# A decoder step in split fp32 matmuls: weights of two or four blocks interleaved column by column, and an activation stored with tokens in falling order

## The chip, the core and the metric

The kernel runs on one core of one Trainium2 chip, as a single launch. The metric is the time of that launch on the device, in microseconds; the times before are two runs of 599.43 and 599.55 us, median 599.49 us. The five engines of the core appear in the profile under short names: PE (TensorE matmuls), PEld (TensorE weight loads, which can run beside PE's matmuls), DVE (VectorE), ACT (ScalarE), POOL (GpSimd); SP is the queue that issues most of the DMAs.

## The reference

One inference step of two layers, for a prompt of 256 tokens and 8 single sample tokens which share all weights. Each layer has a mixer (one input projection, attention beside a second branch, one output projection) and a feed-forward part with a causal convolution of width 3 on its gate. The feed-forward part is what matters here:

```python
def conv_ffn(x, prev, norm_g, w_gate, w_up, conv_w, conv_b, w_down):
    T = x.shape[1]
    h = rmsnorm(x, norm_g)
    g = h @ w_gate
    g_all = jnp.concatenate([prev, g], axis=1)
    gc = sum(conv_w[i] * g_all[:, i:i + T] for i in range(CONV_W)) + conv_b
    a = jax.nn.gelu(gc) * (h @ w_up)
    return x + a @ w_down, g_all[:, -(CONV_W - 1):]
```

The model width is 1024 and the feed-forward width 2816. All inputs and outputs are fp32.

## The kernel before

Features lie on the 128 partitions and tokens along the free dimension: T = 264 columns, 256 of the prompt and 8 samples. Every weight matrix is cut into blocks of 128 x 128. A block is the stationary operand of a matmul and 128 features x 264 tokens are the moving one, so a weight matrix of 1024 x 2816 is 8 x 22 blocks.

To keep fp32 accuracy, each operand is split into two parts of type fp32r: a high part h, which is the value rounded to fp32r, and a low part l, the rest. A block then takes three matmuls into the same PSUM tile: weight h by activation h, weight h by activation l, weight l by activation h. Each of the three loads its own weights.

The list `_PHASES` (from `_phases`) holds eight phases in the order in which they run, and each phase the order of its blocks: `in0`, `out0`, `ff0`, `dn0`, then the same four of layer 1. `ff0` and `ff1` are the gate and up projections (352 blocks each, 1056 matmuls), `dn0` and `dn1` the down projections (176 blocks each, 528 matmuls). Together these four make 1056 of the 1472 blocks.

On the host, `_pack_weights` lays all blocks out in the order of use, in chunks of 8 or 16 blocks. A chunk lies as 128 rows, one for each partition, and in a row the blocks follow each other, 128 columns each. A DMA brings a chunk into a tile `raw`. `split` takes eight blocks at a time, 128 x 1024: ACT writes the high part into a tile `wh` (line 300) and DVE the low part into `wl` (line 303), three such steps ahead of use. In `run`, block i is then the columns `c` to `c + 128` of both tiles, `c = (i % 8) * P`, and the three matmuls are issued (all through a helper at line 215). When a PSUM tile has its last block, `evac` is called.

In `ffn`, the evacuation of a gate block works out the convolution and the GELU on DVE and ACT; that of an up block multiplies on DVE (line 584) and POOL (line 585), and `halves` (ACT line 445, DVE line 446) splits the product into the tiles `a_h` and `a_l`. These are the moving operand of the down phase, which `hl(act, k)` picks for feature block k. Down phases sum over all 22 feature blocks for each of the 8 output blocks; the outputs are added to the residual `X`.

The order of TensorE's instructions is fixed by hand: they keep the order of the program, and the small matmuls of attention and the other branches are hung between blocks as hooks. The feed-forward phases have almost none.

The line that chooses the block's columns, and the three matmuls, are:

```python
            c = (i % 8) * P
            pe.matmul(o, h[:, c:c + P], xh, start=first, stop=False)
            pe.matmul(o, h[:, c:c + P], xl, start=False, stop=False)
            pe.matmul(o, l[:, c:c + P], xh, start=False, stop=left[m] == 0)
```

Of the kernel before, what the change touches and what calls it, by code (L numbers as in the profile page):

```python
# [18 lines left out]
P = 128  # L19
# [39 lines left out]
def _phases():  # L59
    k8 = list(range(KD))  # L60
    in0 = [(n, t) for n in ("bv", "q", "k", "bu", "v") for t in range(4)]
    q0 = [(m, k) for k in range(KQ) for m in in0[:4]] + [(m, k) for m in in0[:4] for k in range(KQ, KD)]
    in1 = [(n, t) for n in ("u", "q", "k", "v") for t in range(4)]
    m8 = [("o", t) for t in range(8)]
    kb = [4, 5, 6, 7, 0, 1, 2, 3]
    ff = [(n, j) for j in range(NF) for n in ("g", "u")]
    kf = list(range(NF))
    ph = []
    for l, ins in enumerate((in0, in1)):
        ph.append((f"in{l}", _split_order(ins, k8, 4) if l else q0 + [(m, k) for m in in0[4:] for k in k8]))  # L70
        ph.append((f"out{l}", _split_order(m8, kb, 4)))
        ph.append((f"ff{l}", _split_order(ff, k8, 4)))
        ph.append((f"dn{l}", [(m, k) for m in m8 for k in kf]))
    return ph


_PHASES = _phases()
# [5 lines left out]
_COLS = {"in0": {"q": 0, "k": 4, "v": 8, "bu": 12, "bv": 16}, "in1": {"q": 0, "k": 4, "v": 8, "u": 12}}  # L83


def _pack_weights(w_in0, w_out0, w_in1, w_out1, gate, up, down):
    def blocks(w):
        kt, mt = w.shape[0] // P, w.shape[1] // P
        return w.reshape(kt, P, mt, P).transpose(2, 0, 1, 3).reshape(mt * kt, P, P), kt

    mats = {"in0": w_in0, "out0": w_out0, "in1": w_in1, "out1": w_out1}
    for l in range(2):
        mats[f"g{l}"], mats[f"u{l}"], mats[f"dn{l}"] = gate[l], up[l], down[l]
    base, kts, parts, n = {}, {}, [], 0
    for name, w in mats.items():
        b, kts[name] = blocks(w)
        base[name] = n
        parts.append(b)
        n += b.shape[0]
    allb = np.concatenate(parts)  # L100
    idx = []
    for ph, order in _PHASES:
        for (n_, t), k in order:
            if ph in _COLS:
                name, m = ph, _COLS[ph][n_] + t
            elif ph.startswith("ff"):
                name, m = n_ + ph[2], t
            else:
                name, m = ph, t
            idx.append(base[name] + m * kts[name] + k)  # L110
    out, o = [], 0
    for c in _CHUNKS:
        out.append(allb[np.array(idx[o:o + c])].transpose(1, 0, 2).reshape(-1))
        o += c
    return out

# [86 lines left out]
def tile_decoder_step(ctx: ExitStack, tc: tile.TileContext, a):  # L203
# [16 lines left out]
    pe = TensorE()  # L220
# [10 lines left out]
    def f4(name, shape=(P, 4, T), dt=F32):  # L231
        return up.tile(list(shape), dt, tag="u", name=name)

    def mv(name):
        return [f4(f"{name}_{x}", dt=F32R) for x in "hl"]

    def hl(tiles, k):
        return tiles[k // 4][0][:, k % 4, :], tiles[k // 4][1][:, k % 4, :]

    def at(name):  # L240
        return psa.tile([P, 512], F32, tag="at", name=name)
# [13 lines left out]
    def vec(n):  # L255
        o, w = _VEC[n]
        return VEC[:, o:o + w]
# [34 lines left out]
    def split(t):  # L292
        for tt in range(len(splits), min(t + (2 if t == 3 else LOOK), NT - 1) + 1):
            ci = chunk_of[tt]
            for c in range(ci, min(ci + 3, len(_CHUNKS))):
                raw(c)
            o = (tt * 8 - coff[ci]) * P
            src = raws[ci][:, o:o + 8 * P]
            h, l = splits[tt] = wtiles(tt)
            i = s.activation(h, src, AF.Copy)  # L300
            if R0 and tt < 8:
                behind(i, last[0])
            i = v.tensor_tensor(l, src, h.bitcast(F32), ALU.subtract)  # L303
            if tt == 5:
                behind(i, summed)
        return splits[t]

    spare = (32, 40)

    def run(order, rhs, evac, hooks=None):  # L310
        hooks = sorted((hooks or {}).items())
        n = 0
        seen, left, ps = {}, {}, {}
        for m, k in order:
            left[m] = left.get(m, 0) + 1
        for m, k in order:
            i = pos[0]
            pos[0] += 1
            h, l = split(i // 8)
            c = (i % 8) * P  # L320
            if m not in ps:
                ps[m] = at(f"mm{i}") if i in spare else psm.tile([P, 512], F32, tag="mm", name=f"mm{i}")
                first = True
            else:
                first = False
            left[m] -= 1
            o = ps[m][:, :T]
            xh, xl = rhs(m, k)
            pe.matmul(o, h[:, c:c + P], xh, start=first, stop=False)
            pe.matmul(o, h[:, c:c + P], xl, start=False, stop=False)  # L330
            if i == 0:
                busy(128)
            pe.matmul(o, l[:, c:c + P], xh, start=False, stop=left[m] == 0)
            if left[m] == 0:
                evac(m, o)
            n += 1
            while hooks and n >= round(8 * (hooks[0][0] + 1)):
                for f in hooks.pop(0)[1]:
                    f()

    orders = dict(_PHASES)
# [9 lines left out]
    first, o = [], 0  # L351
# [26 lines left out]
    def busy(n):  # L378

        tc.keep_in_program_order(pe.matmul(pw[:, :n], warm[:, :P], warm[:, :n], start=True, stop=True))  # L380
# [46 lines left out]
    def rstd_of(parts, scale, name, pin=False, bank=None, w=None):  # L427
        p = (bank or at)(f"ns_{name}")
        for i, x in enumerate(parts):
            mm = pe.matmul(p[:, :T], ones if w is None else w, x, start=i == 0, stop=i == len(parts) - 1)  # L430
            if pin:
                tc.keep_in_program_order(mm)
        R = sm.tile([P, T], F32, tag="R", name=f"R_{name}", bufs=2)
        s.activation(R, p[:, :T], AF.Ln, bias=epst, scale=scale)
        last[0] = s.activation(R, R, AF.Exp, scale=-0.5)
        return R

# [6 lines left out]
    def halves(h, l, src):  # L444
        s.activation(h, src, AF.Copy)  # L445
        v.tensor_tensor(l, src, h.bitcast(F32), ALU.subtract)  # L446
# [82 lines left out]
    def gelu_set():  # L529
        tc.keep_in_program_order(s.preload_act_table_set("gelu_apprx_tanh_and_others"))  # L530
# [4 lines left out]
    def lnexp():  # L535
        tc.keep_in_program_order(s.preload_act_table_set("natural_log_exp_and_others"))
# [15 lines left out]
    def ffn(l, xg, nrm, down_evac, hooks=None):  # L552
        cw, cb = vec("cw"), vec("cb")
        wc = lambda i, j: cw[:, (l * 3 + i) * NF + j:(l * 3 + i) * NF + j + 1]
        cvo = sm.tile([P, NF, 10], F32, tag="cvo", name=f"cvo{l}", bufs=1)
        act = [mv(f"a{l}_{i}") for i in range((NF + 3) // 4)]
        half = {}
        R = None
        nrm.split()

        def norm():
            nonlocal R
            R = nrm.finish()
            gelu_set()


        def evac(m, o):
            n, j = m
            if n == "g":
                wk = f4(f"wk{l}_{j}", (P, 2, T))  # L570
                C = wk[:, 0, :]
                G = wk[:, 1, :]
                v.tensor_tensor(G, o, R, ALU.mult)
                s.activation(C, G, AF.Identity, scale=wc(2, j), bias=cb[:, l * NF + j:l * NF + j + 1])
                v.scalar_tensor_tensor(C[:, 1:SEQ], G[:, 0:SEQ - 1], wc(1, j), C[:, 1:SEQ], ALU.mult, ALU.add)
                v.scalar_tensor_tensor(C[:, 2:SEQ], G[:, 0:SEQ - 2], wc(0, j), C[:, 2:SEQ], ALU.mult, ALU.add)
                v.tensor_tensor(C[:, SEQ:T], C[:, SEQ:T], C0[:, l, j, :], ALU.add)
                s.activation(cvo[:, j, :], G[:, SEQ - 2:T], AF.Copy)
                s.activation(C, C, AF.Gelu_apprx_tanh)
                half[j] = wk  # L580
            else:
                wk = half.pop(j)
                C, A = wk[:, 0, :], wk[:, 1, :]
                v.tensor_tensor(A, o, R, ALU.mult)  # L584
                g.tensor_tensor(A, A, C, ALU.mult)  # L585
                halves(*hl(act, j), A)

        hk = Hooks()
        hk.at(16 / 8 - 1, norm)
        run(orders[f"ff{l}"], pick(xg), evac, hk)  # L590
        nc.sync.dma_start(a[f"cv{l}"], cvo)
        lnexp()
        run(orders[f"dn{l}"], lambda m, k: hl(act, k), down_evac, hooks)

    def residual(gain, name):
        xg = [mv(f"xg_{name}{i}") for i in range(2)]
# [52 lines left out]
    def pick(xg):  # L649
        return lambda m, k: hl(xg, k)  # L650
# [330 lines left out]
    for n in range(8):  # L981
        hk.at(n, drip_of(kload, 2))
    ffn(0, xg, norm_f, evac, hk)


# [95 lines left out]
    U, A, B = [f4(f"pool{x}", (P, 4, PW + SEQ)) for x in "uab"]  # L1081
# [74 lines left out]
    norm_f = nrm  # L1156
    evac, rest = final()
    ffn(1, xg, norm_f, evac)
    rest()

# [68 lines left out]
```

## Time and profile before

| what | value |
|---|---|
| median of two runs | 599.49 us |
| the profiled execution: its time | 599.23 us |
| the profiled execution: span from first to last instruction | 597.2 us |
| `mm` matmuls in a gate and up phase | 1056 each |
| `mm` matmuls in a down phase | 528 each |
| share of ACT, of DVE in the span | 57%, 71% |
| HBM traffic | 117.65 MB read, 3.96 MB written |

The profile is one execution. A row of a group names the line, the engine, the operation, the tile written and those read, the shape and the count; after the bar stand the busy time in us, the mean length of one in ns, and the idle time of the engine just before them with what ended most of it. A row of the timeline gives the start and the length in us. A row of a stretch of time gives its bounds and length, the busy time of PE, PEld, DVE, ACT and POOL with their counts, the granted TensorE clock (1.00 is full), the busy share of the DMA engines, and GB/s. Matmuls are pipelined, so their lengths overlap, and their ends are modelled; the distance between starts is the pace.

### The profile page before, as it was taken

Reading aid. Unit: us, or ns where it says so; the run is one execution under the profiler, and the core shown is the slowest. Engines: PE = TensorE matmul, PEld = TensorE weight load, DVE = VectorE, ACT = ScalarE, POOL = GpSimd, SP = SyncE. Lnnn points to the kernel's source line nnn. Section 1 sums busy time; section 2 is a strip of 40 time slices with the busy share of each in tenths; the row PEclk is TensorE's granted clock in tenths of the full one; section 3 lists DMA queues with packets and bytes.
Section 4 is the critical chain, followed back from the end, with each engine's and each line's share of the span. In section 5 each row is a group of like instructions: output and inputs, shape, how many; then the busy total and the mean of one; then the engine's idle time right before and its main releaser. Section 6 shows DMA issues by size and latency. Waiting matters only on the chain.

```text
span 597.2 us, 12397 instructions
## 1 busy us (share of the span) xinstructions
PE 588.4 (99%) x4907; PEld 570.4 (96%) x4907; DVE 423.4 (71%) x739; ACT 342.5 (57%) x600; POOL 104.8 (18%) x99
## 2 busy tenths in 40 slices
PE   9999999999999999999999999999999999999995
PEld 8999879999999999999999879999999999999994
DVE  7999566877777777655659676687777777864442
ACT  7757845676565655644453556567656565564441
POOL 2100003212313232110120000121232323211110
PEclk9999999999999999999999999999999999999998
DMA  8898844545454545895567763554545454555502
GB/s 334 339 399 348 293 158 156 212 147 204 150 205 153 204 151 202 280 373 201 177 224 278 260 207 97 171 211 148 206 149 206 150 204 156 198 175 198 200 1 74
DMA packets 27707, 122.41 MB, mean 205 GB/s; under 512 B 3330, under 2 KB 4482, under 8 KB 16258
## 3 DMA queue, kind: packets, MB, share of 16 engines
q1 hardware_dynamic: 27072, 120.55, 56.2%
q10 hardware_dynamic: 578, 1.07, 0.5%
q8 instruction: 39, 0.64, 0.4%
q14 instruction: 18, 0.15, 0.1%
HBM read 117.65 MB, written 3.96 MB: 204 GB/s over the span
## 4 chain that ended last, share of the span: by engine, by line
PE 97%; DMA 1%; DVE 1%; ACT 0%; DVEq 0%; issue 0%; SPq 0%
PE mm L215 90%; PE pv_l L215 1%; PE sc L215 1%; PE pav L215 1%; PE pt L218 1%; DMA xw<-in_xw 1%; PE S L215 1%; PE Z L215 1%; PE pf L215 0%; DVE y L643 0%; PE pm L215 0%; PE vtp_v L218 0%; PE po_l L218 0%; PE vtp_sgu L218 0%; PE ns_fin L215 0%; DVE wl L666 0%
## 5 line engine op out<-in xcount | busy, mean ns | idle before, releaser
L303 DVE TENSOR_TENSOR wl<-raw,wh 128x1024 fp32r<-128x1024 f32 x179 | 219.6, 1228 | 74.4 <-ACT wh L300 74.3
L300 ACT ACTIVATE wh<-raw 128x1024 fp32r<-128x1024 f32 x179 | 188.3, 1055 | 90.2 <-PE mm L215 83.3
L215 PE MATMUL mm<-xg_f_h,wh 128*128 128x264 f32 x704 | 200.4, 285 | 0.0
L215 PE MATMUL mm<-xg_f_l,wh 128*128 128x264 f32 x704 | 200.1, 284 | 0.0
L215 PE MATMUL mm<-xg_f_h,wl 128*128 128x264 f32 x704 | 198.9, 283 | 0.0
L215 PEld LDWEIGHTS mm<-xg_f_l,wh 128*128 128x128 f32 x704 | 132.4, 188 | 0.0
L215 PEld LDWEIGHTS mm<-xg_f_h,wh 128*128 128x128 f32 x704 | 132.3, 188 | 0.0
L215 PEld LDWEIGHTS mm<-xg_f_h,wl 128*128 128x128 f32 x704 | 132.3, 188 | 0.0
L585 POOL TENSOR_TENSOR wk<-wk 128x264 f32<-128x264 f32 x44 | 66.2, 1506 | 194.3 <-DVE wk L584 169.0
L215 PE MATMUL mm<-a_h,wh 128*128 128x264 f32 x352 | 100.2, 285 | 0.0
L215 PE MATMUL mm<-a_l,wh 128*128 128x264 f32 x352 | 100.0, 284 | 0.0
L215 PE MATMUL mm<-a_h,wl 128*128 128x264 f32 x352 | 99.5, 283 | 0.0
L215 PEld LDWEIGHTS mm<-a_l,wh 128*128 128x128 f32 x352 | 66.2, 188 | 0.0
L215 PEld LDWEIGHTS mm<-a_h,wh 128*128 128x128 f32 x352 | 66.2, 188 | 0.0
L215 PEld LDWEIGHTS mm<-a_h,wl 128*128 128x128 f32 x352 | 66.1, 188 | 0.0
L445 ACT ACTIVATE a_h<-wk 128x264 fp32r<-128x264 f32 x44 | 18.7, 424 | 73.4 <-POOL wk L585 73.4
L446 DVE TENSOR_TENSOR a_l<-wk,a_h 128x264 fp32r<-128x264 f32 x44 | 19.2, 437 | 41.5 <-ACT a_h L445 41.5
L215 PE MATMUL mm<-xg_h,wh 128*128 128x264 f32 x160 | 47.8, 299 | 0.0
L215 PE MATMUL mm<-xg_h,wl 128*128 128x264 f32 x160 | 45.5, 285 | 0.2 <-DVE wl L666 0.2
L215 PE MATMUL mm<-xg_l,wh 128*128 128x264 f32 x160 | 45.5, 285 | 0.0
L215 PE MATMUL mm<-xg_n_h,wh 128*128 128x264 f32 x128 | 38.5, 301 | 0.0
L215 PE MATMUL mm<-xg_n_l,wh 128*128 128x264 f32 x128 | 36.3, 284 | 0.0
(254 smaller groups left out, 897.7 us busy)
## 6 DMA issues: line engine op xcount, KB each, us to landing
raw<-in_w SPq DMA_DIRECT2D x89, 1024.0 KB, 4.8
K<-in_kt SPq DMA_DIRECT2D x32, 256.0 KB, 6.4
V<-in_vp SPq DMA_DIRECT2D x32, 256.0 KB, 6.9
raw<-in_w SPq DMA_DIRECT2D x4, 512.0 KB, 6.1
X<-in_x SPq DMA_DIRECT2D x4, 264.0 KB, 7.7
xw<-in_xw SPq DMA_DIRECT2D x2, 388.0 KB, 5.4
out_k<-k SPq DMA_DIRECT2D x1, 528.0 KB
out_v<-v SPq DMA_DIRECT2D x1, 528.0 KB, 4.7
```

The lines of the kernel that those rows point to most:

```text
L215: return self.keep(nc.tensor.matmul(*x, **k))
L218: return self.keep(nc.tensor.transpose(*x, **k))
L300: i = s.activation(h, src, AF.Copy)
L303: i = v.tensor_tensor(l, src, h.bitcast(F32), ALU.subtract)
L445: s.activation(h, src, AF.Copy)
L446: v.tensor_tensor(l, src, h.bitcast(F32), ALU.subtract)
L585: g.tensor_tensor(A, A, C, ALU.mult)
```

## The change

Two edits that touch the layout of data only. The first: for three phases the eight blocks of a step are laid out differently in memory. With "pair" (phases `ff0` and `dn0`), two neighbouring blocks are interleaved column by column: column 0 of the first, column 0 of the second, column 1 of the first, and so on, so that the columns of one block are 8 bytes apart. With "four" (phase `ff1`), four blocks are interleaved in the same way, and the columns of one block are 16 bytes apart. The host does the interleaving in `_rows`; the tiles `raw`, `wh` and `wl` have the same size and are still written straight through. `block` picks the columns of block i with the step. All other phases, `dn1` among them, keep the plain layout.

The second: in both layers the product of gate and up is written into `a_h` and `a_l` with its 264 tokens in falling order (`back`), and the down phase reads it with a step of -1, so that its output has the tokens in rising order again.

```diff
+_LAY = {'ff0': 'pair', 'dn0': 'pair', 'ff1': 'four'}
+_LAYT = [_LAY.get(ph) for ph, order in _PHASES for _ in range(len(order) // 8)]
+
+def _rows(b, lay):
+
+    if lay == "pair":
+        return b.reshape(4, 2, P, P).transpose(2, 0, 3, 1).reshape(P, -1)
+    if lay == "four":
+        return b.reshape(2, 4, P, P).transpose(2, 0, 3, 1).reshape(P, -1)
+    return b.transpose(1, 0, 2).reshape(P, -1)
...
     for c in _CHUNKS:
-        out.append(allb[np.array(idx[o:o + c])].transpose(1, 0, 2).reshape(-1))
+        out.append(np.concatenate([_rows(allb[np.array(idx[t:t + 8])], _LAYT[t // 8]) for t in range(o, o + c, 8)], 1).reshape(-1))
...
+    def block(w, i):
+
+        j, lay = i % 8, _LAYT[i // 8]
+        if lay == "pair":
+            return w.rearrange("p (j c b) -> p j c b", c=P, b=2)[:, j // 2, :, j % 2]
+        if lay == "four":
+            return w.rearrange("p (j c b) -> p j c b", c=P, b=4)[:, j // 4, :, j % 4]
+        return w[:, j * P:(j + 1) * P]
...
-            c = (i % 8) * P
+            h, l = block(h, i), block(l, i)
...
-            pe.matmul(o, h[:, c:c + P], xh, start=first, stop=False)
-            pe.matmul(o, h[:, c:c + P], xl, start=False, stop=False)
+            pe.matmul(o, h, xh, start=first, stop=False)
+            pe.matmul(o, h, xl, start=False, stop=False)
...
-            pe.matmul(o, l[:, c:c + P], xh, start=False, stop=left[m] == 0)
+            pe.matmul(o, l, xh, start=False, stop=left[m] == 0)
...
+        def back(k):
+            return [x[:, ::-1] for x in hl(act, k)]
...
-                halves(*hl(act, j), A)
+                halves(*back(j), A)
...
-        run(orders[f"dn{l}"], lambda m, k: hl(act, k), down_evac, hooks)
+        run(orders[f"dn{l}"], lambda m, k: back(k), down_evac, hooks)
```

## The prediction, made before the changed kernel ran

> **What bounds the kernel now.** I read the page first: the busy shares, the granted clock by slice, the chain of work that ended last.
>
> ```profile
> span 597.2 us, 12397 instructions
> PE 588.4 (99%) x4907; PEld 570.4 (96%) x4907; DVE 423.4 (71%) x739; ACT 342.5 (57%) x600; POOL 104.8 (18%) x99
> PEclk9999999999999999999999999999999999999998
> PE 97%; DMA 1%; DVE 1%; ACT 0%; DVEq 0%; issue 0%; SPq 0%
> ```
>
> TensorE is the kernel: 97% of the chain, at the full granted clock. Matmuls overlap, so a busy share of 99% does not say what sets their pace. Next I read the busy time by stage. The four stretches are the two gate and up phases (first and third row) and the two down phases (second and fourth). After the length of a stretch stand busy time and count per engine.
>
> ```profile
> 112.90:241.00 128.10, 128.10 (x1060) 128.10 (x1059) 97.44 (x173) 75.81 (x134) 32.42 (x23) 1.00 0.50 177
> 241.00:304.90 63.90, 63.90 (x530) 63.90 (x529) 38.54 (x44) 31.78 (x42) 8.44 (x11) 1.00 0.72 260
> 396.40:524.50 128.10, 128.10 (x1060) 128.10 (x1060) 97.42 (x173) 75.64 (x134) 32.88 (x23) 1.00 0.50 177
> 524.50:588.50 64.00, 64.00 (x531) 64.00 (x530) 29.29 (x34) 29.45 (x39) 9.21 (x7) 1.00 0.38 133
> ```
>
> 128.10 / 1060 is 120.8 ns a matmul, and 63.90 / 530 is 120.6. The pace is the same with DVE at 97 of 128 us or at 29 of 64, and with the DMA share at 0.38 or 0.72: nothing outside TensorE slows these phases. They hold 384 of the 597 us, and they are where the change acts. What makes 121 ns is in the timeline of a gate and up phase (start, duration, instruction), and in the groups of weight loads of different width.
>
> ```profile
> 210.13 0.28 PE L215 MATMUL mm<-xg_f_h,wh 128*128 128x264 f32 x1
> 210.14 0.19 PEld L215 LDWEIGHTS mm<-xg_f_l,wh 128*128 128x128 f32 x1
> 210.25 0.28 PE L215 MATMUL mm<-xg_f_l,wh 128*128 128x264 f32 x1
> 210.26 0.19 PEld L215 LDWEIGHTS mm<-xg_f_h,wl 128*128 128x128 f32 x1
> 210.37 0.28 PE L215 MATMUL mm<-xg_f_h,wl 128*128 128x264 f32 x1
> ```
>
> ```profile
> L215 PEld LDWEIGHTS mm<-xg_f_l,wh 128*128 128x128 f32 x704 | 132.4, 188 | 0.0
> L215 PEld LDWEIGHTS pav<-pT,vt 128*64 128x64 f32 x64 | 4.8, 136 | 0.8 <-issue 0.2
> L215 PEld LDWEIGHTS sc<-K,qz_l 128*32 128x32 f32 x128 | 4.0, 110 | 2.7
> ```
>
> A weight load begins 0.01 us after the matmul before it, and its own matmul begins 0.11 us later. The widths give 110, 136 and 188 ns for 32, 64 and 128 columns: 0.81 ns a column, so 128 x 0.81 = 104 ns of a full load is the reading of columns. The transposes show the same unhidden: six loads of 128 columns back to back, with matmuls of 128 columns.
>
> ```profile
> 46.38 0.69 PEld L218 LDWEIGHTS pt<-CST,p 128*128 128x128 f32 x6
> 46.49 0.82 PE L218 MATMUL pt<-CST,p 128*128 128x128 f32 x6
> ```
>
> (0.69 - 0.14) / 5 = 0.11 us a load, 0.14 being the length of the last one by its group below. So I read 121 ns as a ring: start of matmul, 0.01, load of 0.11, next matmul. The load is on the path. The streaming of 264 columns takes at most 0.121 us, so 0.46 ns a column or less, and may be on the path as well.
>
> ```profile
> L218 PEld LDWEIGHTS pt<-CST,p 128*128 128x128 f32 x24 | 2.8, 140 | 0.0
> ```
>
> **The change part by part.** Instructions, their order on every engine and their waits are the same in the two programs; only addresses differ. So no queue moves, no wait is added, and DMAs carry the same bytes to the same tiles in the same packets. Splitting a tile of weights (ACT and DVE, 128x1024) still runs straight through it. Three things are left.
>
> 1. Stationary operand in steps of 8 bytes ("pair"): 1056 loads in the first gate and up phase and 528 in the first down phase, 1584 in all. No row of this kernel reads weights in steps, so I bound it by the speed at which a read sweeps addresses. The plain load sweeps 4 bytes in 0.81 ns, 4.9 bytes a ns; the moving operand sweeps 4 bytes in 0.46 ns or less, at least 8.7 bytes a ns, and that is shown to work. "Pair" at 0.81 ns a column needs 9.8 bytes a ns. Lower end: free. Upper end: a cap at exactly 8.7, so 8 / 8.7 = 0.92 ns a column, 14 ns a load, 22 us. [...] I take free, because the sweep is within 13% of one that is shown and that is itself only a lower bound.
>
> 2. Stationary operand in steps of 16 bytes ("four"): 1056 loads in the second gate and up phase. It needs 19.7 bytes a ns, 2.3 times anything shown. Lower end: free. Upper end, with the cap at 8.7: 1.84 ns a column, 132 ns more a load, 139 us. I take a doubling, the value that goes with "pair" being just free: 104 ns x 1056 = 109.8 us. As the load is on the ring, nothing covers it. If the 121 - 104 = 17 ns that are not column reading could overlap the longer load, 87 ns x 1056 = 91.9 us remain.
> [...]
>
> 3. Falling order of tokens. Written by 22 ACT and 22 DVE instructions in each layer, read as the moving operand of 528 matmuls in each down phase.
>
> ```profile
> L445 ACT ACTIVATE a_h<-wk 128x264 fp32r<-128x264 f32 x44 | 18.7, 424 | 73.4 <-POOL wk L585 73.4
> L446 DVE TENSOR_TENSOR a_l<-wk,a_h 128x264 fp32r<-128x264 f32 x44 | 19.2, 437 | 41.5 <-ACT a_h L445 41.5
> L584 DVE TENSOR_TENSOR wk<-mm,R_f 128x264 f32<-128x264 f32 x44 | 19.0, 432 | 5.0
> L585 POOL TENSOR_TENSOR wk<-wk 128x264 f32<-128x264 f32 x44 | 66.2, 1506 | 194.3 <-DVE wk L584 169.0
> L1021 DVE TENSOR_TENSOR_SCAN keep<-keep,edge 128x383 f32<-128x383 f32 x8 | 7.5, 950 | 3.7 <-ACT keep L1019 3.7
> L1022 DVE TENSOR_TENSOR w<-w,keep 128x384 f32<-128x384 f32 x8 | 4.3, 553 | 0.4
> ```
>
> The only falling rows are the scans (L1021): 950 ns against 553 for a plain product of the same length, 1.72 times, though a scan may cost that in either direction. At worst L445 and L446 take 1.72 times as long, 0.62 us a block of features. They have cover: the last block is ready 0.43 + 1.51 + 0.42 + 0.44 = 2.8 us after its last matmul, 3.4 us at the worst, and the down phase uses it as its 22nd, after 21 x 3 x 0.121 = 7.6 us. DVE would be busy 22 x 0.31 = 7 us longer in a phase with 31 us to spare. So nothing for the writing. Reading: lower end free; upper end, one column in the time that the load takes for one, 264 x 0.81 = 214 ns, 93 ns over the pace, or 110 if the 17 ns add, x 1056 = 99 to 116 us. The factor 1.72 on the ring gives 92 us. I take free: the addresses are the same consecutive ones.
>
> Sum against the profiled execution, which took 599.23 us (span 597.2 and 2.0 around it; the median of the two runs is 599.49, 0.04% more): 599.2 + 0 + 109.8 + 0 = 709 us. With the bounds of term 2 alone 691 (91.9) to 738 (139); I let its own range end at 720, as a cap at 8.7 would need the streaming to fill the whole ring.
>
> **The rivals.**
>
> - No change: a load gets a fresh 16 bytes every 0.81 ns without waiting. Place: the second gate and up phase; it decides if the sweep may reach 19.7 bytes a ns. For it: the weight port is read here at only 4.9 bytes a ns, half of what the moving port shows, so spare speed exists. Against: no row goes beyond 8.7. All terms are 0: 599 us. [...]
> - Falling order halves the stream, the steps are free: 599.2 + 99 to 116 = 698 to 715 us. For it: the moving operand is read nearly twice as fast as the weights, so it may be fetched several columns at a time in rising order. Against: only the scan shows a falling row, and not TensorE's.
> - Both "four" and falling order cost: 709 + 99 to 116 = 808 to 825 us.
> - Every step over 4 bytes doubles the load, "pair" too: 2640 x 104 = 275 us, 874; with falling order as well some 980.
> [...]
>
> **How the numbers follow.** "Four" alone 0.50; no change 0.22; falling order alone 0.08; both 0.08; "pair" and "four" 0.06; everything 0.02; faster 0.04. The first three make 0.80, so the range goes from the unchanged time, 598, to the end of the likeliest case, 720; the likeliest case's own range is 691 to 720. A measurement of this kernel tells about 2% from no change. Slower by over 2%: 0.50 + 0.08 + 0.08 + 0.06 + 0.02 = 0.74; within 2%: 0.22; faster: 0.04. The predicted time is the likeliest case's, 709 us.
>
> **What would show it.** In the changed kernel the second gate and up phase should last about 238 us instead of 128 with the same 1060 matmuls (225 ns each), its weight loads should be some 104 ns longer than 188, and DVE and ACT should wait there for TensorE. The first gate and up phase should keep 128 us, and the two down phases 64 each. A first down phase that is longer while the first gate and up phase isn't would speak for falling order, and the second down phase, which has falling order alone, would settle it. All four at 121 ns would make the prediction wrong: then the weight port has speed to spare.

## The result, and the profile after

The changed kernel takes 721.4 us (two runs, 721.08 and 721.67) against 599.5 us: 1.204 times as long, with a 95% interval of 1.202 to 1.206. The profiled execution took 721.67 us, with a span of 719.7 us.

The page of the changed kernel, busy shares, granted clock and chain:

```profile
span 719.7 us, 12397 instructions
PE 711.1 (99%) x4907; PEld 693.1 (96%) x4907; DVE 426.9 (59%) x739; ACT 344.5 (48%) x600; POOL 100.2 (14%) x99
PEclk9999999999999999999999999999999999999999
PE 96%; DMA 1%; DVE 1%; ACT 1%; issue 0%; DVEq 0%
```

The counts are the same, the granted clock is at 90% or more in every slice, and DVE and ACT are busy for nearly the same time as before (426.9 for 423.4 us, 344.5 for 342.5). Nothing was added but time on TensorE, and its busy share, 99% in both kernels, does not show it. The stretches do. The four phases in the order of before, with the same columns:

```profile
113.10:244.00 130.90, 130.90 (x1060) 130.90 (x1058) 99.67 (x176) 77.03 (x136) 31.06 (x23) 1.00 0.51 180
244.10:308.00 63.90, 63.90 (x530) 63.90 (x528) 36.76 (x41) 30.65 (x39) 8.27 (x11) 1.00 0.68 245
399.60:646.60 247.00, 247.00 (x1059) 247.00 (x1058) 103.10 (x178) 78.49 (x136) 30.25 (x23) 1.00 0.27 96
646.90:710.90 64.00, 64.00 (x528) 64.00 (x528) 26.88 (x28) 28.17 (x36) 9.02 (x7) 1.00 0.33 116
```

Cut from the first to the last matmul's start in the same way, the phases of before last 128.0, 63.8, 128.0 and 63.8 us. So the second gate and up phase ("four") lost 119.0 us, the first ("pair") 2.9, the first down phase (pair and falling order) 0.1 and the second (falling order alone) 0.2. Together 122.2 of the 122.5 us by which the span grew. The weight loads of the second and of the first gate and up phase of the changed kernel, from the groups of each stretch:

```profile
L229 PEld LDWEIGHTS mm<-xg_f_h,wh 128*128 128x128 f32 x352 | 116.2, 330 | 0.0
```

```profile
L229 PEld LDWEIGHTS mm<-xg_f_h,wh 128*128 128x128 f32 x352 | 68.9, 196 | 0.0
```

188 ns became 330 with four and 196 with pair. The timeline of the second gate and up phase shows what the ring of before turned into:

```profile
499.97 0.40 PE L229 MATMUL mm<-xg_f_h,wl 128*128 128x264 f32 x1
500.07 0.33 PEld L229 LDWEIGHTS mm<-xg_f_h,wh 128*128 128x128 f32 x1
500.21 0.40 PE L229 MATMUL mm<-xg_f_h,wh 128*128 128x264 f32 x1
500.30 0.33 PEld L229 LDWEIGHTS mm<-xg_f_l,wh 128*128 128x128 f32 x1
500.44 0.40 PE L229 MATMUL mm<-xg_f_l,wh 128*128 128x264 f32 x1
```

Starts of matmuls are 0.23 to 0.24 us apart. A load now begins 0.09 to 0.10 us after the start of the matmul before it, no longer 0.01, and its own matmul 0.14 us later. The matmuls are recorded 0.11 us longer too (a mean of 398 ns for 285), though they stream the same 264 columns, so the cost is read from the distance of the starts and not from a recorded length.

### The profile page after: what moved, and what is told of

It reads as the page before. It is cut to its first block, busy times and chain, and to the rows that moved or that the text cites. A ratio compares the mean times of both kernels' runs of the same rounds, so it can differ in the third digit from the quotient of the medians.

```text
span 719.7 us, 12397 instructions
## 1 busy us (share of the span) xinstructions
PE 711.1 (99%) x4907; PEld 693.1 (96%) x4907; DVE 426.9 (59%) x739; ACT 344.5 (48%) x600; POOL 100.2 (14%) x99
## 4 chain that ended last, share of the span: by engine, by line
PE 96%; DMA 1%; DVE 1%; ACT 1%; issue 0%; DVEq 0%
PE mm L229 90%; PE pv_l L229 1%; DMA raw<-in_w 1%; PE sc L229 1%; PE pav L229 1%; PE pt L232 1%; PE S L229 1%; PE Z L229 0%; DMA xw<-in_xw 0%; PE pf L229 0%; ACT wh L700 0%; DVE y L670 0%; PE pm L229 0%; PE vtp_v L232 0%; PE po_l L232 0%; DVE wl L701 0%
## 5 line engine op out<-in xcount | busy, mean ns | idle before, releaser
L314 ACT ACTIVATE wh<-raw 128x1024 fp32r<-128x1024 f32 x179 | 189.8, 1061 | 245.4 <-PE mm L229 239.3
L229 PE MATMUL mm<-xg_f_l,wh 128*128 128x264 f32 x704 | 242.1, 344 | 0.0
L229 PE MATMUL mm<-xg_f_h,wh 128*128 128x264 f32 x704 | 241.1, 342 | 0.0
L229 PE MATMUL mm<-xg_f_h,wl 128*128 128x264 f32 x704 | 239.1, 340 | 0.0
L229 PEld LDWEIGHTS mm<-xg_f_h,wl 128*128 128x128 f32 x704 | 186.0, 264 | 0.0
L229 PEld LDWEIGHTS mm<-xg_f_l,wh 128*128 128x128 f32 x704 | 185.6, 264 | 0.0
L229 PEld LDWEIGHTS mm<-xg_f_h,wh 128*128 128x128 f32 x704 | 185.1, 263 | 0.0
L612 POOL TENSOR_TENSOR wk<-wk 128x264 f32<-128x264 f32 x44 | 61.9, 1409 | 316.2 <-ACT wk L606 262.3
L611 DVE TENSOR_TENSOR wk<-mm,R_f 128x264 f32<-128x264 f32 x44 | 19.0, 432 | 52.8 <-PE mm L229 50.3
L600 DVE TENSOR_TENSOR wk<-mm,R_f 128x264 f32<-128x264 f32 x44 | 18.9, 430 | 44.9 <-PE mm L229 44.9
```

The lines of the kernel that those rows point to most:

```text
L229: return self.keep(nc.tensor.matmul(*x, **k))
```

## The experiments

Every experiment is a kernel of its own, run once with a profile beside a run of the kernel before on the same chip (599.70 or 599.75 us). One run is enough for what is read here: in all of them the phases that were left as before last 128.0 or 128.1 and 63.8 or 63.9 us, except in `e7_half`; `e8_falls` leaves none as it was. The pace of a phase is its length divided by its 1056 or 528 matmuls.

**Each edit alone.** `e1_four` keeps only four, `e2_pair` only pair, `e3_fall` only the falling order.

```diff
-_LAY = {'ff0': 'pair', 'dn0': 'pair', 'ff1': 'four'}
+_LAY = {'ff1': 'four'}                       # e1_four
+_LAY = {'ff0': 'pair', 'dn0': 'pair'}        # e2_pair
+_LAY = {}                                    # e3_fall
...
-            return [x[:, ::-1] for x in hl(act, k)]
+            return hl(act, k)                # e1_four, e2_pair
```

> Only the interleaving by four in the second gate and up phase is kept; weights elsewhere are plain and tokens rise. In the changed kernel that phase ran at 234.1 ns a matmul against 121.3 before, so (234.1 - 121.3) ns x 1056 = 119.1 us. Theory 'four alone': 599.2 + 119 = 718 us, the phase again 247 us. Rival 'the three edits add to each other' (falling order before it, or the steps of the first layer, lengthen the phase): clearly less than 718.

> Only the interleaving by two in the first gate and up phase and the first down phase is kept; tokens rise. The changed kernel lost 2.8 ns a matmul in the first of these phases and 0.1 in the second, where tokens also fell. Theory 'pair leaves no spare': both phases lose about 2.8 ns, 2.9 + 1.5 = 4.4 us, 604 us, and it was falling order that healed the second phase. Rival 'the moving tiles of the gate and up phase collide with pair, those of the down phase don't': 2.9 us and 0, 602 us. Rival 'free': 599 us.

> Only the falling order of tokens in both down phases is kept; all weights are plain. The second down phase of the changed kernel, which has falling order alone, lost 0.5 ns a matmul. Theory 'falling order is read like rising order': 599.5 us, both down phases within 0.3 us of 63.8. Rival 'it cost something that pair hid in the first down phase': that phase over 65 us.

718.79, 603.27 and 600.34 us. First the second gate and up phase of `e1_four`, then the two phases with pair of `e2_pair`, then the two down phases of `e3_fall`:

```profile
396.90:643.90 247.00, 247.00 (x1059) 247.00 (x1058) 103.02 (x178) 78.37 (x136) 30.20 (x23) 1.00 0.27 96
```

```profile
112.70:243.60 130.90, 130.90 (x1059) 130.90 (x1058) 99.72 (x176) 76.84 (x136) 30.98 (x23) 1.00 0.50 178
243.70:308.90 65.20, 65.20 (x530) 65.20 (x529) 36.95 (x41) 30.62 (x39) 8.30 (x11) 1.00 0.69 243
```

```profile
241.70:305.80 64.10, 64.10 (x530) 64.10 (x529) 38.46 (x44) 31.78 (x42) 8.39 (x11) 1.00 0.71 259
525.50:589.60 64.10, 64.10 (x529) 64.10 (x528) 29.17 (x34) 29.44 (x39) 9.18 (x7) 1.00 0.37 132
```

Four alone makes the whole 119.0 us in its phase: the theory "four alone" holds. Pair costs in both of its phases, 2.9 and 1.4 us, so the 0.1 us in the changed kernel's first down phase was two edits together: pair and falling order cost 0.1 us there, pair alone 1.4. Falling order alone costs 0.3 us in each down phase.

**A longer step.** `e4_eight` interleaves all eight blocks in the second gate and up phase, so that columns are 32 bytes apart.

```diff
+    if lay == "eight":
+        return b.transpose(1, 2, 0).reshape(P, -1)
...
+        if lay == "eight":
+            return w.rearrange("p (c b) -> p c b", b=8)[:, :, j]
```

> As the kernel before, but in the second gate and up phase eight blocks are interleaved, so that the columns of a block are 32 bytes apart. [...] Rival 'sweep', which the prediction used: the read is limited in bytes of address per ns, so twice the step takes twice the time: 0.81 ns a column became about 1.7 at 16 bytes and becomes about 3.4, 334 ns more a load than plain, 599 + 353 = some 950 us.

727.33 us. The phase:

```profile
397.10:652.50 255.40, 255.40 (x1059) 255.40 (x1058) 102.94 (x178) 78.35 (x136) 30.21 (x23) 1.00 0.26 93
```

255.40 us / 1056 is 242 ns a matmul. Twice the step of four, which ran at 234, costs 8 ns more, where "sweep" wanted some 220 more. The limit in bytes of address per ns, with which the prediction sized both steps, falls. What the 8 ns are, no run shows.

**A step between.** `e5_three` interleaves blocks as 3 + 3 + 2 in the same phase.

```diff
+    if lay == "three":
+        return np.concatenate([x.transpose(1, 2, 0).reshape(P, -1) for x in (b[0:3], b[3:6], b[6:8])], 1)
...
+        if lay == "three":
+            n, e = j // 3, min(j // 3 * 3 + 3, 8)
+            return w[:, n * 3 * P:e * P].rearrange("p (c b) -> p c b", b=e - 3 * n)[:, :, j % 3]
```

> As the kernel before, but in the second gate and up phase the eight blocks of a step are interleaved as 3 + 3 + 2, so that columns are 12 bytes apart in six blocks and 8 bytes in two. Theory 'line': a load costs its number of 16-byte pieces, 1.69 ns each (0.81 ns a column plus the 112.8 / 128 that 'four' added): 96 pieces at 12 bytes, 162 ns against 104 plain, 58 ns more; with 2.8 ns for the two blocks 44 ns on the mean, 46.7 us, 646 us. Rival 'threshold': below 16 bytes all is nearly free as with pair: 602 us. Rival 'any odd step pays like four': 6/8 of 119 us, 689 us.

642.97 us, near the 646 of "line" and far from the 602 and 689 of its rivals; the phase takes 171.7 us, 163 ns a matmul, 41 more than plain where "line" said 44. The timeline shows the six loads of a group of two blocks (from 450.55) between loads of groups of three; rows left out are marked:

```profile
450.37 0.26 PEld L231 LDWEIGHTS mm<-xg_f_h,wl 128*128 128x128 f32 x1
450.55 0.21 PEld L231 LDWEIGHTS mm<-xg_f_h,wh 128*128 128x128 f32 x1
450.68 0.20 PEld L231 LDWEIGHTS mm<-xg_f_l,wh 128*128 128x128 f32 x1
...
451.29 0.25 PEld L231 LDWEIGHTS mm<-xg_f_h,wh 128*128 128x128 f32 x1
451.46 0.26 PEld L231 LDWEIGHTS mm<-xg_f_l,wh 128*128 128x128 f32 x1
...
452.51 0.26 PEld L231 LDWEIGHTS mm<-xg_f_l,wh 128*128 128x128 f32 x1
```

From 451.46 to 452.51 there are six distances (left out there are five loads of 0.26 or 0.27): 0.175 us each at 12 bytes. From 450.68 to 451.29 there are five (left out are four loads of 0.19 or 0.20), 0.122 each, at 8 bytes. So the cost does not set in at 16 bytes only: 12 bytes have about half of it. By the step the pace is 124 ns a matmul at 8 bytes, 175 at 12, 234 at 16 and 242 at 32 (`e2_pair`, `e5_three`, `e1_four`, `e4_eight`): 51 and 59 ns for 4 bytes more each, and only 8 ns for the next 16. "Line" counts pieces of 16 bytes of address, 64, 96, 128 and 128 in a load of 128 columns, and these paces put 1.6 to 1.8 ns on each piece from 64 to 128. Such a price is the author's estimate, worked out from these four paces; no run shows a piece, or shifts the start of a block within 16 bytes.

**The load, or load and stream in turn?** In `e7_half` the second gate and up phase has four, and the second and third matmul of each block of both gate and up phases stream 132 columns instead of 264, which leaves out the small terms of the other tokens.

```diff
+            n_ = TH if 'ff' in _PHOF[i] else T
-            pe.matmul(o, h, xl, start=False, stop=False)
+            pe.matmul(o[:, :n_], h, xl[:, :n_], start=False, stop=False)
...
-            pe.matmul(o, l, xh, start=False, stop=left[m] == 0)
+            pe.matmul(o[:, :n_], l, xh[:, :n_], start=False, stop=left[m] == 0)
```

> The second gate and up phase has four, all else is as before, but in both gate and up phases the second and the third matmul of each block stream only the first 132 tokens (the small terms of tokens 132 to 263 are left out there). Theory 'the load alone sets the ring', plain and with four: pace stays 121 and 234 ns, 718 us. Rival 'load and stream take turns at the memory': a matmul that streams 132 columns less saves 132 x 0.42 = 55 ns, x 704 in each phase, 39 us each, 640 us. Rival 'in the plain layout the stream is the longer one': the first phase falls towards the 110 ns of the transposes after short matmuls, up to 11 ns x 704 = 8 us, and the second stays: 710 us.

717.40 us. The two gate and up phases; the third figure from the end is the granted clock:

```profile
112.70:234.20 121.50, 121.50 (x1060) 121.50 (x1058) 94.34 (x167) 73.75 (x131) 29.14 (x22) 1.00 0.52 181
392.50:641.90 249.40, 249.40 (x1060) 249.40 (x1058) 102.77 (x178) 78.14 (x136) 28.61 (x23) 0.51 0.27 95
```

The total is near the 718 of the first theory, but by chance. The plain phase saved 6.5 us; 2.4 were lost in the phase with four, and 2.8 and 0.8 in the two down phases (66.6 and 64.6 us), in the first of which TensorE is idle for 1.9 us (busy 64.7).

In the plain phase, at a clock of 1.00, the 6.5 us are near the 8 of the third theory: with plain weights the stream counts too, 115 ns a matmul with half of it left out in two of three, 121 with all. That they take turns is out there: it wanted 39 us.

With four, streaming half the columns in two of three matmuls saves nothing, 249.4 us for 247.0. But the granted clock fell to 0.51 in this phase, where `e1_four` had 1.00; why, no run shows. So the time of the phase does not separate the stream from the clock. Its timeline does:

```profile
499.89 0.33 PEld L230 LDWEIGHTS mm<-xg_f_l,wh 128*128 128x128 f32 x1
500.09 0.33 PE L230 MATMUL mm<-xg_f_l,wh 128*128 128x132 f32 x1
500.13 0.33 PEld L230 LDWEIGHTS mm<-xg_f_h,wl 128*128 128x128 f32 x1
500.22 0.44 PE L230 MATMUL mm<-xg_f_h,wl 128*128 128x132 f32 x1
500.37 0.33 PEld L230 LDWEIGHTS mm<-xg_f_h,wh 128*128 128x128 f32 x1
500.45 0.55 PE L230 MATMUL mm<-xg_f_h,wh 128*128 128x264 f32 x1
```

The loads begin 0.24 us apart, though the matmuls begin 0.13 and 0.23 apart and a load begins 0.04 us after one and 0.15 after the next. So with four the loads follow each other at a pace of their own, with 264 or 132 columns streamed beside them, and don't take turns with the stream. This pace is nearly the same at a clock of 0.51 as at 1.00: 236 and 234 ns a matmul.

**Falling order beside pair and four.** `e8_falls` stores the moving operand of both gate and up phases in falling order too, gives the first gate and up phase pair and the three others four, and leaves rising order to the second down phase alone.

```diff
+_LAY = {'ff0': 'pair', 'dn0': 'four', 'ff1': 'four', 'dn1': 'four'}
...
+        if fall:
+            h, l = h[:, ::-1], l[:, ::-1]
...
-            return [x[:, ::-1] for x in hl(act, k)]
+            return hl(act, k) if l else [x[:, ::-1] for x in hl(act, k)]
...
-        run(orders[f"ff{l}"], pick(xg), evac, hk)
+        run(orders[f"ff{l}"], lambda m, k: [x[:, ::-1] for x in hl(xg, k)], evac, hk)
```

> Both gate and up phases and the first down phase read the moving operand with tokens in falling order, the second down phase in rising order; weights are pair in the first gate and up phase and four in the three others. Pair with rising tokens cost 2.8 ns a matmul in both of its phases, with falling ones 0.1. Theory 'the two reads disturb each other when they run in opposite directions': the first gate and up phase is back at 128.0 to 128.6 us, and four with falling tokens loses less than the 112.8 ns that it loses with rising ones: by the 6 ns by which 234 exceeds twice 107 + 14, about 228 ns; four in the second down phase 234 ns; in all 599.5 + 56 + 113 + 59.5 = 828 us. Rival 'four is bound by its own fetches alone': falling order changes nothing there, 599.5 + 112.8 ns x 2112 = 838 us.

838.65 us, as the rival "bound by its own fetches alone" had it. The two gate and up phases (first and third row) and the two down phases:

```profile
113.30:241.30 128.00, 128.00 (x1060) 128.00 (x1059) 97.31 (x173) 75.93 (x134) 32.34 (x23) 1.00 0.50 178
241.40:365.00 123.60, 123.60 (x529) 123.60 (x528) 38.98 (x44) 31.81 (x42) 8.56 (x11) 1.00 0.39 142
456.80:704.30 247.50, 247.50 (x1058) 247.50 (x1058) 103.02 (x178) 78.61 (x136) 30.16 (x23) 1.00 0.27 96
704.60:827.80 123.20, 123.20 (x528) 123.20 (x528) 27.06 (x28) 28.16 (x36) 9.03 (x7) 1.00 0.17 60
```

Pair with falling tokens is free in a gate and up phase as well, 128.0 us: the small cost of pair shows only beside a rising stream (130.9 us). Four is as dear with falling tokens (123.6 and 247.5 us) as with rising ones (123.2, and 247.0 in `e1_four`). So the first theory is right on pair and wrong on four. In which direction a load runs, no record shows, so "opposite directions" was not shown.

**Steps in the moving operand.** `e6_moving` leaves all weights plain and interleaves feature blocks token by token, two in the first down phase, four in the second. `e9_runs` does the same in runs of two adjacent tokens, and addresses the output of these matmuls in pairs of tokens too (those edits are not shown). `e10_both` has the first down phase of `e6_moving` and weights in four there.

```diff
+            n = (2, 4)[l]                    # e6_moving, e9_runs; e10_both: (2, 1)[l]
+            i, b = (k % 4) // n * n, k % n
+            return [x.rearrange("p f t -> p (f t)")[:, i * T:(i + n) * T].rearrange("p (t b) -> p t b", b=n)[:, :, b] for x in act[k // 4]]
...
+            return [x.rearrange("p f t -> p (f t)")[:, i * T:(i + n) * T].rearrange("p (t b e) -> p t b e", b=n, e=2)[:, :, b, :] for x in act[k // 4]]   # e9_runs
```

> Weights are plain everywhere and tokens rise, but the moving operand of the down phases is interleaved: in the first layer two feature blocks token by token (tokens 8 bytes apart), in the second four (16 bytes apart). Theory 'line, the same on both ports': 132 and 264 pieces at 1.69 ns, 223 and 446 ns for the stream of one matmul; with the load no longer the longer of the two, pace about 225 to 235 and 446 to 460 ns against 121, +57 and +175 us, some 830 us. Rival 'the moving port fetches pieces twice as fast' (0.85 ns): first down phase free, second about 225 to 235 ns, 656 us. Rival 'steps matter to weights only': 600 us.

> All weights are plain and tokens rise. The moving operand of the down phases lies in runs of two adjacent tokens: in the first layer two feature blocks alternate (runs 16 bytes apart), in the second four (32 bytes apart). With single tokens 8 and 16 bytes apart both phases had run at 236 and 240 ns a matmul, so the step did not matter, only that there was one. Theory 'the moving port takes two adjacent tokens at a time': runs of two cost little, both phases within 3 us of 63.8, 600 us. Rival 'what counts are 16-byte pieces, 1.69 ns each': 132 pieces in both, 223 ns and more, both phases about 124 us, 720 us.

> Only the first down phase differs from the kernel before: its weights are interleaved by four (16 bytes apart; alone 234 ns a matmul) and its moving operand token by token by two (8 bytes apart; alone 236 ns). Theory 'the load and the stream run side by side, each with its own reading': the longer one sets the pace, 236 to 245 ns, 600 + 63 = 662 us. Rival 'they share the reading': the losses add, 121 + 113 + 115 = 349 ns, 720 us.

722.85, 722.79 and 661.88 us. The two down phases of `e6_moving`, those of `e9_runs`, and the first of `e10_both`:

```profile
241.10:365.50 124.40, 124.40 (x529) 109.51 (x528) 39.09 (x44) 31.88 (x42) 8.61 (x11) 1.00 0.40 142
585.40:711.90 126.50, 126.50 (x530) 109.50 (x529) 32.64 (x39) 31.54 (x42) 10.73 (x8) 1.00 0.20 70
```

```profile
241.10:365.60 124.50, 124.50 (x530) 109.58 (x529) 39.13 (x44) 31.96 (x42) 8.60 (x11) 1.00 0.39 141
585.50:711.90 126.40, 126.40 (x528) 109.36 (x528) 29.90 (x34) 29.78 (x40) 9.17 (x7) 1.00 0.19 67
```

```profile
240.90:367.40 126.50, 126.50 (x530) 126.50 (x528) 39.18 (x44) 31.95 (x42) 8.62 (x11) 1.00 0.39 139
```

The moving operand takes 236 ns a matmul with two blocks interleaved and 240 with four, token by token (8 and 16 bytes) or in runs of two. Weight loads are idle for 15 to 17 us in these phases: here the stream, not the load, is the bound. All three theories of `e6_moving` fall: at 8 bytes it isn't free, and at 16 bytes it does not double again. Two adjacent tokens don't help, so the theory of `e9_runs` falls too, unless the pairs in the output cost just as much, which was not tried alone. Its rival gives the right time there, but cannot be the cause: at 1.69 ns a piece, 264 pieces in the second phase of `e6_moving` would have taken 446 ns. In all four phases the moving operand in steps took 236 to 240 ns a matmul, some 0.9 ns a column (240 / 264), about half the speed of the one that lies straight (at most 0.46 ns, 121 / 264). Runs longer than two tokens were not tried.

`e10_both` is plain: a load of 234 ns and a stream of 236 make 240 together, not 349. The two run side by side.

None of these kernels is faster than the kernel before.

## Why the prediction was wrong, by its own steps

The time, 721.4 us, lies above the range, which ended at 720, and the likeliest case's time, 709, was 12.4 us short. The path was the right one: four alone slows the weight load, nothing covers it, and DVE and ACT wait (ACT's splitting waited 239.3 us in all for TensorE, by the list of waits of the changed kernel, against 83.3 before). The step that failed is the size of terms 1 and 2: four at 104 ns a load where 112.7 were measured (9.2 us), and pair at nothing where it cost 2.9 us. With 0.3 us for falling order this is the whole 12.4. Either alone would have left the time in the range: `e1_four`, with nothing but four, took 718.79.

- **What bounds the kernel.** Right that the load is on the path and that nothing outside TensorE counts. But with four there is no longer a ring of matmul and load: in `e7_half` the loads keep their distance of 0.24 us, with matmuls 0.13 and 0.23 apart. For the plain layout "may be on the path as well" was the right caution: 6.5 us went with half the stream.
- **Term 2, four.** "I take a doubling, the value that goes with 'pair' being just free: 104 ns" was mis-sized: 119.0 us / 1056 = 112.7 ns, 9.2 us more than the 109.8 of the sum. The derivation failed with it: 104 came from a limit in bytes of address per ns, which `e4_eight` rejects (242 ns, not some 450), so it was luck that it came within 9 ns. The runs put a price by the step in its place: 234 - 124 = 110 ns from 8 to 16 bytes, and 8 ns from 16 to 32. By the estimate in pieces of 16 bytes, four has 64 more than pair, 1.7 ns each, on top of the 2.8 ns of pair.
- **The end of the range.** The working had an upper end for term 2 of 139 us, 738 in all, and then let the range stop at 720 on the ground that a cap at 8.7 bytes a ns would need the streaming to fill the ring. That stop rested on the same limit and left no room for pair, and the range missed the time by 1.4 us.
- **Term 1, pair.** "I take free" left out 2.9 us, inside the 22 that bounded it. That falling order would hide the same cost in the first down phase was not foreseen.
- **Term 3, falling order.** Right: 0.3 us in each down phase alone. The writes kept their length, 425 ns on ACT and 435 on DVE (424 and 437 before), so the factor 1.72 of the scans did not carry over.
- **The rivals.** "No change" and "falling order" are ruled out by `e1_four` and `e3_fall`; "pair too" by `e2_pair` (4.3 us in its two phases, 3.6 in all over its 599.7); no phase with steps and full matmuls took less than the 128.0 or 63.8 us of before, so a gain, to which the chances gave 0.04, is out too.
- **What would show it.** The phase of 238 us came out at 247, the loads at 330 ns instead of 292; the other three phases were called right to 3 us.

What stays open: why pair and a rising stream cost 2.8 ns together and pair and a falling one nothing; the last 8 ns of `e4_eight`; and why the moving operand pays the same at every step.

## What to carry to other kernels

Where weight loads set TensorE's pace, as here, the layout of the weights is on the path in full: keep the columns of a stationary fp32 block adjacent (121 ns a matmul here), or at most 8 bytes apart (124); 12 bytes took 175 and 16 bytes 234. The moving operand is less forgiving: here each of the four layouts in steps, 8 bytes included, cost about as much as weights 16 bytes apart (236 to 240 ns for 234), while falling order cost 0.3 us in a phase of 64. A busy share of 99% told nothing in either kernel; the distance between starts did (0.12 us before, 0.23 to 0.24 with four).

## What was not expected of the hardware

- The load with four kept its pace at a granted clock of 0.51 (249.4 us with half the streaming, against 247.0 at 1.00): this stage, bound by loads, did not slow by more than 1% when the clock was taken back.
- Stepped loads and a stepped stream do not add: 240 ns together, 234 and 236 apart.
- The moving operand in steps of 8 bytes takes 236 ns, though two tokens lie in each 16 bytes; weights in steps of 8 bytes take 124.
